# Issuing the transfers of the inverted 64-blocks from GpSimd's queue instead of SyncE's

## The chip, the core and the metric

The kernel runs on one core of a Trainium2 chip. The core has five engines with an instruction queue each: TensorE (PE; its weight loads are listed apart as PEld), ScalarE (ACT), VectorE (DVE), GpSimd (POOL) and SyncE (SP). A transfer between the chip's memory (DRAM) and the core's on-chip memory is an instruction in the queue of one engine; that engine issues it, in the order of its queue and after the waits that stand before it, and 16 DMA engines then carry it out. The metric is the device time of one execution in microseconds (us).

## What is computed

One step of a decoder of two layers, for a prompt of 512 tokens and 8 sampled tokens at once. Layer 0 mixes by a convolution and by attention; layer 1, in which the change lies, is a gated delta net with 16 query/key heads and 32 value heads. Its prompt part works on chunks of 64 tokens, 8 chunks for each value head, and for each of them it inverts a lower triangular matrix of 64 x 64:

```python
lmat = jnp.where(strict, jnp.einsum('bhnid,bhnjd->bhnij', kb, kc) * decay, 0.0)
tmat = lax.linalg.triangular_solve(lmat + eye, jnp.broadcast_to(eye, lmat.shape),
                                   left_side=True, lower=True, unit_diagonal=True)
u_val = tmat @ (vc * bc[..., None])
w_key = tmat @ (kb * jnp.exp(gc)[..., None])
# per chunk n, with state s:
v_new = u_n - w_n @ s
o_n = qd_n @ s + a_n @ v_new
s = s * gl_n[..., None, None] + jnp.swapaxes(kd_n, -1, -2) @ v_new
```

These are 32 x 8 = 256 matrices, the 64-blocks of the title. The 8 sampled tokens go through the same recurrence one step at a time, each with a state of its own (`state_delta`). All values are fp32.

## The kernel before

The weights stream from DRAM in halves of 128 x 1024 values (`wr`). ACT rounds each half to a short form `wh`, DVE takes the rest, `wl<-wr,wh`, and PE multiplies both by the activations, which are split in the same way (`uh`, `ul`), into `pg`: three products of 16 matmuls of 260 columns for a half, so that a half needs one ACT rounding and one DVE split before its last 16 matmuls.

All instructions are first recorded by a class `Sched`. Its `flush` (lines 307 to 432) then plays the recorded work through: each engine has a clock, `cost` prices an instruction, `LAT` the way from one engine to another, and whenever an engine is free it takes the ready instruction with the lowest number (an order of priority: record order plus a bias). The work is emitted in the order of the planned starts, so every engine's queue is fixed before the run. Transfers are planned on the engine "SP" (`Q` in `build`): an issue costs 340 to 1700 ns, moves on one common clock of transfers (`dma_free`), and SP is held back when that clock is over `WINDOW`, 5 us, ahead.

Layer 1 has two phases. In the first (`l1a`), `prepare(i, lk)` runs for 16 pairs of value heads, i = 0 to 15; it forms the triangular matrices `lt` of the pair and stores them, with the other matrices of the chunks, in a DRAM tile `sp` (`sv` and `spa` are views of it). Behind i = 7 the function `inverses(0, iv)` is recorded for the first eight pairs, the first half; `inverses(1, iv)`, the second half, is a generator that `background` steps forward while the next phase runs.

`inverses` works as follows. Eight loads (`m<-sp`) bring the 128 matrices of its half into a tile `m`, one matrix on each of the 128 partitions, 64 x 64 values each; a load fills 16 partitions, 256 KB, and reads rows of 64 values, so pieces of 256 bytes. DVE puts ones on the diagonals (`MEMSET m` 128x64), then inverts by steps of a multiplication into `tmp` and a sum (`TENSOR_REDUCE`), and at last clears the upper corner (`MEMSET m` 128x32x32, in the trace 128x1024). Eight stores (`sp<-m`) of 256 KB write the inverses back into the places of `lt`. There is one buffer for `m`: the second half's loads wait until the first half's stores have read it.

The second phase (`l1b`) runs for the 16 pairs: `values(i)` (a convolution, `conv_c`, with DVE's steps `cacc<-buf,conv_w_c,cacc`; GpSimd clears the first three columns of each `buf`), `z_gates(i)`, `scan(i, ...)` (it loads the inverses and the other matrices of a pair as `pk<-sp`, 448 KB, and goes through the chunks on PE: `pm`, `ct`, `at`), and `samples(i, ...)`, which loads the sampled tokens' state `S<-state_delta`, copies into one of two tiles `es` that GpSimd cleared at the phase's beginning, and multiplies `pd<-S,es`. `window` loads the small tiles `win`. The output blocks y of the pairs are stored, and towards the end they are loaded again (`m<-y_0`, `m<-y_1`, ...) into the tile `m`, which takes the place of the second half's `m` and so waits for its stores.

Lines 430 and 431 of the profile are the two lines in `flush` that emit every instruction, so its rows tell the work by tile names. The names that the text uses, apart from those above: `z<-dd` (stores of gates from a tile of the first phase; the tiles of the second phase take that room, and the clears of `es` wait for them), `zt<-z` (their loads), `oss` and `vs` (small tiles of the second phase), `kql<-` (the rest of the split of keys and queries in `prepare`), `o_ccp` and `o_ccs` (outputs: the last rows of the convolution's input).

Of the kernel before, what the change touches and what calls it, by code (L numbers as in the profile page):

```python
# [27 lines left out]
GQ = 16  # L28
# [10 lines left out]
class Sched:  # L39


    def __init__(self, tc):
        self.tc, nc = tc, tc.nc
        self.ops, self.rings, self.owner, self.hist, self.masks = [], {}, {}, {}, {}
        self.bias, self.done, self.start, self.fins, self.dma_free, self.aset = 0, 0, [], [], 0.0, 0
        self.real = {"PE": nc.tensor, "ACT": nc.scalar, "DVE": nc.vector, "POOL": nc.gpsimd, "SP": nc.sync}
        self.t = {e: 0.0 for e in self.real}
        self.cols, self.port = [0.0] * 4, {"DVE": 0.0, "POOL": 0.0}

# [192 lines left out]
    def cost(self, eng, meth, args, kw, out, ins):  # L242

        n = self.free(out)
        PSM = bass.MemoryType.PSUM
        big = [x for x in ins if not (self.free(x) == 1 and n > 1)]
        ptr = len(ins) - len(big)
        nps = sum(1 for x in ins if x.space == PSM)
        acc = kw.get("accum_out") is not None
        if eng == "PE":  # L250
            k, m = ins[0].shape[0], out.shape[0]
            rows = 32 if k <= 32 else 64 if k <= 64 else 128
            if meth == "transpose":
                return max(109 if rows == 128 else 82, 0.833 * n + 2), (rows, 128), "t"
            if ins[1].dtype == F32R:
                return (max(120, 0.417 * n + 6) if rows == 128 else 0.833 * n + 8), (rows, 128), "r"
            cols = 32 if m <= 32 else 64 if m <= 64 else 128
            if (rows, cols) == (128, 32):
                return max(100, 1.667 * n + 52), (rows, cols), "q"
            return 2 * max(109 if rows == 128 else 58, 0.833 * n + 3), (rows, cols), "f"  # L260
        if eng == "ACT":
            f = args[2] if meth == "activation" else AF.Copy
            return 0.83 * n + (58 if nps else 109) + 93 * ptr + 105 * acc, f
        if eng == "SP":
            by, run = int(4 * np.prod(out.shape)), 4096
            for x in [out] + ins:
                r = 1
                for st, c in reversed([tuple(d) for d in (x.ap if x.space == bass.MemoryType.DRAM else list(x.ap)[1:])]):
                    if st != r:
                        break  # L270
                    r *= c
                run = min(run, 4 * r)
            few = any(x.space != bass.MemoryType.DRAM and x.shape[0] <= 16 for x in [out] + ins) and by > 20000
            return (1700 if few else 340 if by / run <= 130 else 560), int(by * (1 + 77 / run if run >= 512 else 512 / max(run, 64)))
        two = sum(1 for x in big if x.space != PSM) > 1
        if eng == "DVE":
            fast = meth in ("tensor_scalar", "tensor_copy") and not nps and out.space != PSM
            if meth == "memset":
                return 0.52 * n + 60, True
            if meth == "reciprocal":  # L280
                return 6.6 * n + 70, False
            if meth == "tensor_tensor_scan":
                return 2.09 * n + 55, two
            if meth == "tensor_reduce":
                return 1.04 * self.free(ins[0]) + 65, False
            r = 0.52 if fast else 1.04
            if meth == "tensor_tensor" and n >= 100:
                inner = [[d for d in list(x.ap)[1:] if d[1] > 1] for x in big]
                if any(d and abs(d[-1][0]) > 4 for d in inner):
                    r = 1.83  # L290
            return r * n + 68 + 60 * ptr + 12 * acc, two or fast
        if meth == "tensor_tensor":
            return 1.57 * n + 430, True
        if meth == "tensor_reduce":
            return 2.1 * self.free(ins[0]) + 100, True
        if meth == "memset":
            return 0.5 * n + 130, True
        return 0.83 * n + 370 + 60 * ptr, True
# [3 lines left out]
           "ACT": {"PE": 262, "ACT": 145, "DVE": 132, "POOL": 172},  # L302
           "DVE": {"PE": 257, "ACT": 130, "DVE": 128, "POOL": 157},
           "POOL": {"PE": 205, "ACT": 77, "DVE": 70, "POOL": 90},
           "SP": {"PE": 970, "ACT": 950, "DVE": 950, "POOL": 950, "SP": 1000}}

    def flush(self):

# [8 lines left out]
        for i in range(lo, N):  # L317
            eng, deps, after = ops[i][0], ops[i][5], ops[i][8]
# [17 lines left out]
        while left:  # L336
# [10 lines left out]
            now, e = best  # L347
# [27 lines left out]
            if e == "PE":  # L375
                if c[1] != self.cfg:
                    if self.kind == "q":
                        now = max(now, max(self.cols))
                    now += self.SWITCHED if c[1] == (128, 128) else self.SWITCHES
                    self.cfg = c[1]  # L380
                elif self.kind in "tf" and c[2] == "r":
                    now = max(now - 78, ready[i])
                self.kind = c[2]
                if c[2] == "q":
                    g = self.column(ops[i])
                    start[i] = max(now, self.cols[g])
                    self.cols[g] = fin = start[i] + c[0]
                    end = start[i] + 14
                else:
                    start[i] = now  # L390
                    end = fin = now + c[0]
            elif e == "ACT":
                start[i] = now
                end = fin = now + c[0]
                s = self.SETS.get(c[1])
                if s is not None and self.aset not in s:
                    self.aset = min(s)
                    end = fin = end + 1280
            elif e == "SP":
                start[i] = now  # L400
                end = now + c[0] + 60
                self.dma_free = fin = max(self.dma_free, end + 650) + c[1] / self.RATE
            else:
                other = "POOL" if e == "DVE" else "DVE"
                if c[1]:
                    now = max(now, self.port[other])
                start[i] = now
                end = fin = now + c[0]
                if c[1]:
                    self.port[e] = end  # L410
# [12 lines left out]
        with self.tc.manual_schedule():  # L423
            for i in order:
                o = ops[i]
                s = self.SETS.get(o[6][1]) if o[0] == "ACT" else None
# [70 lines left out]
def build(tc, a, ctx):  # L497
    nc = tc.nc
    sc = Sched(tc)
    V, S, G, PE, Q = (sc.engine(e) for e in ("DVE", "ACT", "POOL", "PE", "SP"))  # L500
    PS = bass.MemoryType.PSUM
    DR = bass.MemoryType.DRAM

# [738 lines left out]
    with ExitStack() as l1:  # L1242
# [122 lines left out]
        def inverses(b8, iv):  # L1365
# [6 lines left out]
                        c0, r = 4 * (8 * b8 + i), slice(64 * blk, 64 * blk + 64)  # L1372
                        blocks.append((m[p0:p0 + 16], spa[c0:c0 + 16, r, 5 + hd, r]))
            for s, dv in blocks:
                Q.dma_start(s, dv)
            mf = m.rearrange("p j i -> p (j i)")
            V.memset(mf[:, 0::65], 1.0)
            pr = m[:, 32:64, 0:32]
# [37 lines left out]
                    yield dot(diag(0, s_, s_ + i, 1, 2 * s_, nb)[:, :, :, 0], x, prb(0, s_, 0, i + 1))  # L1416
            V.memset(pr, 0.0)
            for s, dv in blocks:
                Q.dma_start(dv, s)


        def gates(gp_):
# [518 lines left out]
```

## Time and profile before

| | us |
|---|---|
| median of three timed runs | 3222.65 |
| lowest and highest | 3216.93 and 3229.28 |
| profiled execution, its own time | 3229.8 |
| span of the trace in it | 3228.0 |
| PE busy in the span | 3072.7 (95%) |
| VectorE busy | 2346.4 (73%) |
| ScalarE busy | 1578.2 (49%) |
| GpSimd busy | 128.3 (4%) |

The profile shows one execution. Times are in us from the start of its span. A row of a timeline gives start, duration, engine (SPq is SyncE's queue of transfers), line, operation, output<-inputs and, in brackets, how long the engine was idle before it and which work ended the wait. The duration of a transfer's row on SPq is the time that its issue took; the time until its data has landed is told apart. The duration of a row of several instructions (x6) is that of all of them. PEclk is the granted clock of TensorE as a share of the full one: of the two levels of 1.2 and 2.4 GHz, 1.00 is the higher one throughout. Near 1830 us the first half's inversion ends and near 1865 us the second phase begins; near 2370 us the second half's inversion ends.

### The profile page before, as it was taken

How to read it: one execution, taken by the hardware profiler on the slowest of the kernel's cores; microseconds unless marked ns; L12 is line 12 of the kernel's file. 1: busy time of each engine (PE TensorE's matmuls, PEld its weight loads, DVE VectorE, ACT ScalarE, POOL GpSimd, SP SyncE). 2: the span in 40 equal slices, each digit the busy share in tenths (PEclk: the TensorE clock that was granted, in tenths of full speed). 3: DMA queues.
4: the chain of work that ended last, by engine and by line, in shares of the span. 5: the costliest groups of instructions: out<-in, count | busy, mean ns of one | idle time of the engine just before them, and what ended most of it. 6: DMA issues, size and time to landing. Idle time of an engine off the chain costs nothing.

```text
span 3228.0 us, 65519 instructions
## 1 busy us (share of the span) xinstructions
PE 3072.7 (95%) x24448; PEld 2800.0 (87%) x24448; DVE 2346.4 (73%) x6470; ACT 1578.2 (49%) x2942; POOL 128.3 (4%) x157
## 2 busy tenths in 40 slices
PE   8999999998979999999999979999999989999997
PEld 5798888886868886998999969999989779989997
DVE  3477988789674476676999749999956566665755
ACT  3234344433543366777773236555535555554544
POOL 0000000000001111000000000000000000001111
PEclk9999999999979999999999989999989789899998
DMA  9988898989627798687664485555364444476754
GB/s 316 296 274 292 298 313 293 327 306 316 219 89 260 287 308 276 141 168 149 151 155 135 110 153 176 154 150 168 127 180 146 137 126 154 130 247 193 227 181 137
DMA packets 361586, 667.01 MB, mean 207 GB/s; under 512 B 103698, under 2 KB 216339, under 8 KB 357171
## 3 DMA queue, kind: packets, MB, share of 16 engines
q1 hardware_dynamic: 361266, 662.82, 67.4%
q8 instruction: 192, 3.15, 0.4%
q14 instruction: 128, 1.04, 0.1%
HBM read 574.95 MB, written 87.70 MB: 205 GB/s over the span
## 4 chain that ended last, share of the span: by engine, by line
PE 84%; DVE 7%; DMA 6%; ACT 1%; SPq 1%; issue 1%; POOLq 0%; ACTq 0%; POOL 0%; DVEq 0%
PE pg L431 66%; PE pm L431 9%; PE pl L431 6%; PE pd L431 2%; SPq L431 1%; DVE wl L431 1%; DVE junk L431 1%; DMA S<-state_delta 1%; DMA page<-cache_k 1%; DMA wa<-w_ada 1%; DVE blk L431 1%; DVE acc L431 1%; DVE S L431 1%; DMA o_ds<-S 1%; DMA m<-sp 0%
## 5 line engine op out<-in xcount | busy, mean ns | idle before, releaser
L431 PE MATMUL pg<-uh,wh 128*128 128x260 f32 (+1 forms) x6112 | 1343.3, 290 | 12.5 <-ACT wh L431 6.2
L431 PE MATMUL pg<-ul,wh 128*128 128x260 f32 (+1 forms) x6112 | 1344.0, 289 | 3.0 <-DVE ul L431 2.6
L431 PEld LDWEIGHTS pg<-uh,wh 128*128 128x128 f32 (+1 forms) x6112 | 1001.0, 191 | 67.1 <-issue 46.0
L431 PEld LDWEIGHTS pg<-ul,wh 128*128 128x128 f32 (+1 forms) x6112 | 1004.0, 191 | 46.0 <-issue 33.8
L431 ACT CAST wh<-wr 128x1024 fp32r<-128x1024 f32 (+3 forms) x508 | 512.5, 1010 | 769.0 <-PE pg L431 634.2
L431 PE MATMUL pg<-uh,wl 128*128 128x260 f32 (+1 forms) x6112 | 880.6, 287 | 0.2
L431 DVE TENSOR_TENSOR wl<-wr,wh 128x1024 fp32r<-128x1024 f32 (+3 forms) x508 | 616.0, 1213 | 328.1 <-ACT wh L431 145.6
L431 PEld LDWEIGHTS pg<-uh,wl 128*128 128x128 f32 (+1 forms) x6112 | 791.6, 190 | 42.4 <-issue 37.3
L431 DVE SCALAR_TENSOR_TENSOR junk<-page,qbc 128x128 f32<-128x128 f32 x1024 | 223.2, 293 | 7.7 <-DMA page<-cache_k 4.4
L431 DVE TENSOR_TENSOR tmp<-m 128x224 f32<-128x224 f32 (+19 forms) x238 | 200.8, 844 | 4.0
L431 DVE SCALAR_TENSOR_TENSOR acc<-gp,conv_w_a,acc 128x512 f32<-128x512 f32 x240 | 181.5, 756 | 4.1 <-ACT acc L431 1.1
L431 ACT ACT_TABLE_LOAD x123 | 157.8, 1283 | 22.5 <-DVE rs L431 10.9
L431 DVE SCALAR_TENSOR_TENSOR cacc<-buf,conv_w_c,cacc 128x512 f32<-128x512 f32 x192 | 143.2, 746 | 13.8 <-ACT cacc L431 12.0
L431 DVE TENSOR_REDUCE m<-tmp 128x32 f32<-128x224 f32 (+19 forms) x238 | 131.1, 551 | 4.0
L431 DVE DVE_READ_ACCUMULATOR junk<-page,qbc 128x1 f32 x1024 | 90.2, 88 | 0.0
L431 PE MATMUL pl<-page,wst 128*32 128x512 f32 x512 | 80.2, 611 | 8.8 <-DMA page<-cache_v 8.8
L431 PE MATMUL pl<-wa,cpad 128*32 128x512 f32 x512 | 82.9, 604 | 2.7 <-DMA wa<-w_ada 2.7
L431 PE MATMUL pg<-yh,wh 128*128 128x260 f32 x320 | 79.2, 284 | 0.7 <-ACT wh L431 0.7
L431 PE MATMUL pg<-yl,wh 128*128 128x260 f32 x320 | 78.9, 283 | 0.0
L431 DVE SCALAR_TENSOR_TENSOR S<-S,egb,pl 128x128 f32<-128x128 f32 x256 | 71.9, 341 | 5.7 <-PE pl L431 5.2
L431 ACT ACTIVATE jk<-osb 128x128 f32<-128x128 f32 x128 | 39.7, 310 | 54.9 <-DVE osb L431 53.9
L430 ACT ACT_TABLE_LOAD x51 | 65.4, 1283 | 0.9
(381 smaller groups left out, 3418.8 us busy)
## 6 DMA issues: line engine op xcount, KB each, us to landing
wr<-w_in_odd SPq DMA_DIRECT2D x194, 512.0 KB, 4.6
page<-cache_k SPq DMA_DIRECT2D x128, 512.0 KB, 5.5
wa<-w_ada SPq DMA_DIRECT2D x128, 512.0 KB, 5.4
page<-cache_v SPq DMA_DIRECT2D x128, 512.0 KB, 5.7
wr<-w_out_odd SPq DMA_DIRECT2D x128, 512.0 KB, 3.7
wr<-w_in_even SPq DMA_DIRECT2D x94, 512.0 KB, 5.5
page<-w_ada SPq DMA_DIRECT2D x128, 256.0 KB, 5.0
pk<-sp SPq DMA_DIRECT2D x64, 448.0 KB, 4.0
```

Source lines behind the costliest of these rows:

```text
L430: self.tc.nc.scalar.preload_act_table_set("natural_log_exp_and_others")
L431: o[2](*o[3], **o[4])
```

## The change

The planner gets a sixth engine, "GQ", which stands for transfers issued from GpSimd's queue: a clock of its own, the price and the latencies of SP, but no holding back by `WINDOW`. In `inverses`, and only there, the eight loads and the eight stores of a half are recorded on it (`Q2`) instead of on SP (`Q`). At run time they stand in GpSimd's one queue together with its other instructions, in the planned order.

```diff
-        self.real = {"PE": nc.tensor, "ACT": nc.scalar, "DVE": nc.vector, "POOL": nc.gpsimd, "SP": nc.sync}
+        self.real = {"PE": nc.tensor, "ACT": nc.scalar, "DVE": nc.vector, "POOL": nc.gpsimd, "SP": nc.sync, "GQ": nc.gpsimd}
...
-        if eng == "SP":
+        if eng in ("SP", "GQ"):
...
-           "SP": {"PE": 970, "ACT": 950, "DVE": 950, "POOL": 950, "SP": 1000}}
+           "SP": {"PE": 970, "ACT": 950, "DVE": 950, "POOL": 950, "SP": 1000, "GQ": 1000}}
+    LAT["GQ"] = LAT["SP"]
...
-            elif e == "SP":
+            elif e in ("SP", "GQ"):
...
-    V, S, G, PE, Q = (sc.engine(e) for e in ("DVE", "ACT", "POOL", "PE", "SP"))
+    V, S, G, PE, Q, Q2 = (sc.engine(e) for e in ("DVE", "ACT", "POOL", "PE", "SP", "GQ"))
...
             for s, dv in blocks:
-                Q.dma_start(s, dv)
+                Q2.dma_start(s, dv)
             mf = m.rearrange("p j i -> p (j i)")
...
             for s, dv in blocks:
-                Q.dma_start(dv, s)
+                Q2.dma_start(dv, s)
```

With other engines and clocks the planner comes to another order at some places. On GpSimd, from the middle of the first phase on, before:

```order
L431 TENSOR_TENSOR blk<-blk,rows 128x2x260 x10
L431 MEMSET buf 128x3 x32
L431 MEMSET es_25415 128x256
L431 MEMSET es_25416 128x256
L431 MEMSET buf 128x3 x32
```

and now, up to the second half's loads:

```order
L432 MEMSET buf 128x3 x11
L432 DMA m<-sp 16x64x64 x4
L432 MEMSET buf 128x3 x8
L432 DMA m<-sp 16x64x64 x4
L432 MEMSET buf 128x3 x13
L432 DMA sp<-m 16x64x64 x8
L432 DMA m<-sp 16x64x64
L432 MEMSET es_25415 128x256
L432 MEMSET es_25416 128x256
L432 MEMSET buf 128x3 x2
L432 DMA m<-sp 16x64x64 x7
L432 MEMSET buf 128x3 x16
```

The first half's stores and one load of the second half stand ahead of the clears of `es`, and seven loads ahead of the next clear of `buf`; the second half's eight stores follow further down. The first of the second half's loads carries the wait for the stores to have landed.

On VectorE, at the beginning of the second phase, before (the copies into `es` are those of the first two pairs, `MEMSET m` is the second half's diagonal):

```order
L431 COPY es_25416<-kqd 128x8 x2
L431 TENSOR_TENSOR wl<-wr,wh 128x1024 x2
...
L431 TENSOR_TENSOR vs<-pm,snk 128x512
L431 TENSOR_TENSOR wl<-wr,wh 128x1024 x2
L431 COPY win<-pg 128x8
L431 TENSOR_TENSOR wm<-win,conv_w_c 128x64
L431 SCALAR_TENSOR_TENSOR cacc<-buf,conv_w_c,cacc 128x512
L431 TENSOR_REDUCE dv<-wm 128x16
L431 SCALAR_TENSOR_TENSOR cacc<-buf,conv_w_c,cacc 128x512 x2
L431 TENSOR_TENSOR wl<-wr,wh 128x1024
L431 TENSOR_TENSOR vs<-pm,snk 128x512
L431 MEMSET m 128x64
```

and now:

```order
L432 TENSOR_TENSOR vs<-pm,snk 128x512
L432 TENSOR_TENSOR wl<-wr,wh 128x1024
L432 MEMSET m 128x64
L432 TENSOR_TENSOR tmp<-m 128x8
...
L432 TENSOR_REDUCE m<-tmp 128x8x4
L432 COPY win<-pg 128x8
L432 TENSOR_TENSOR tmp<-m 128x200
L432 TENSOR_TENSOR wl<-wr,wh 128x1024
L432 SCALAR_TENSOR_TENSOR cacc<-buf,conv_w_c,cacc 128x512
```

The clear of `m`, which waits for all eight loads, comes behind one weight split where it came behind three, and the three `cacc` steps that were ahead of it stand behind it.

On SyncE, where the second half's stores were, before:

```order
L431 DMA wr<-w_in_odd 128x1024
L431 DMA sp<-m 16x64x64 x3
L431 DMA wr<-w_in_odd 128x1024
L431 DMA sp<-m 16x64x64 x3
L431 DMA wr<-w_in_odd 128x1024
L431 DMA sp<-m 16x64x64
L431 DMA pk<-sp 128x896 x3
```

and now:

```order
L432 DMA S<-state_delta 128x2048
L432 DMA wr<-w_in_odd 128x1024
L432 DMA pk<-sp 128x896
L432 DMA zt<-z_17859 128x520
L432 DMA m<-y_0_17875 128x260
L432 DMA m<-y_1_17876 128x260
L432 DMA wr<-w_in_odd 128x1024
L432 DMA m<-y_2_17877 128x260
```

The stores are gone from this queue; the `pk` here is that of pair 8, the first one that reads the second half's inverses (it waits for four of the stores), and the loads of y into `m` (which wait for the other four) stand close behind it, each group with a weight load after it.

## Rows read from the trace of the kernel before

**Rows 1.** The page: busy time, share of the span and instructions of each engine.

```profile
PE 3072.7 (95%) x24448; PEld 2800.0 (87%) x24448; DVE 2346.4 (73%) x6470; ACT 1578.2 (49%) x2942; POOL 128.3 (4%) x157
```

**Rows 2.** The page: the chain that ended last, share of the span by engine.

```profile
PE 84%; DVE 7%; DMA 6%; ACT 1%; SPq 1%; issue 1%; POOLq 0%; ACTq 0%; POOL 0%; DVEq 0%
```

**Rows 3.** Stretches: length; busy us (instructions) of PE, PEld, DVE, ACT, POOL; PEclk, DMA share, GB/s.

```profile
1530.00:1830.00 300.00, 298.17 (x2493) 296.45 (x2492) 294.61 (x550) 161.30 (x228) 1.11 (x11) 1.00 0.53 140
1838.00:1856.00 18.00, 18.00 (x153) 18.00 (x151) 3.67 (x3) 4.29 (x5) 0.00 (x0) 1.00 0.76 113
1875.00:1887.00 12.00, 10.35 (x86) 10.36 (x87) 5.76 (x10) 4.16 (x6) 0.00 (x0) 1.00 1.21 108
1890.00:1920.00 30.00, 15.73 (x109) 12.02 (x108) 7.46 (x19) 5.29 (x15) 0.10 (x1) 0.70 1.00 130
2400.00:2420.00 20.00, 20.00 (x101) 17.20 (x102) 1.92 (x4) 5.06 (x16) 0.20 (x2) 0.56 0.65 183
```

**Rows 4.** Timeline of SyncE's queue between the phases: start, us, operation.

```profile
1838.10 17.84 SPq L431 DMA_DIRECT2D sp<-m  x6
1856.04 5.34 SPq L431 DMA_DIRECT2D z<-dd  x2
...
1874.59 12.36 SPq L431 DMA_DIRECT2D m<-sp  x3
...
1902.92 3.05 SPq L431 DMA_DIRECT2D S<-state_delta  x1
```

**Rows 5.** Timeline of VectorE at the same place.

```profile
1832.94 0.91 DVE L431 MEMSET m<- 128x1024 f32 x1 [0.16 <-issue]
...
1851.45 1.23 DVE L431 TENSOR_TENSOR wl<-wr,wh 128x1024 fp32r<-128x1024 f32 x1 [4.55 <-PE pg L431]
...
1864.68 0.10 DVE L431 MEMSET oss<- 128x10 f32 x2 [12.01 <-DMA z<-dd]
...
1913.77 0.11 DVE L431 MEMSET m<- 128x64 f32 x1 [22.16 <-DMA m<-sp]
```

**Rows 6.** Timeline of PE at the same place.

```profile
1868.28 0.80 PE L431 MATMUL pg<-uh,wh 128*128 128x260 f32 x2 [5.37 <-ACT wh L431]
...
1887.60 2.09 PE L431 MATMUL pg<-uh,wl 128*128 128x260 f32 x16
...
1916.17 1.93 PE L431 MATMUL pd<-S,es 128*32 128x256 f32 x16 [10.33 <-DMA S<-state_delta]
```

**Rows 7.** Timeline of GpSimd: near the first loads, and between the phases.

```profile
1402.16 0.10 POOL L431 MEMSET buf<- 128x3 f32 x1 [22.19 <-DVE lt L431]
...
1864.66 0.56 POOL L431 MEMSET es<- 128x256 f32 x2 [199.57 <-DMA z<-dd]
...
1888.69 0.10 POOL L431 MEMSET buf<- 128x3 f32 x1 [23.38 <-DMA o_ccp<-buf]
```

**Rows 8.** Timelines of SyncE, VectorE and PE at the first half's last loads.

```profile
1485.83 0.33 SPq L431 DMA_DIRECT2D m<-sp  x1
...
1503.68 0.11 DVE L431 MEMSET m<- 128x64 f32 x1 [9.19 <-DMA m<-sp]
...
1507.00 0.58 PE L431 MATMUL pm<-kql,kqh 128*128 128x256 f32 x1 [7.72 <-DVE kql L431]
```

**Rows 9.** Timelines of SyncE and PE at the second half's stores.

```profile
2369.02 7.74 SPq L431 DMA_DIRECT2D sp<-m  x3
...
2390.54 3.98 SPq L431 DMA_DIRECT2D pk<-sp  x3
...
2397.10 0.42 PE L431 MATMUL pm<-ct,pk 64*64 64x64 f32 x2 [4.49 <-DMA pk<-sp]
```

**Rows 10.** Tile m: issue ns (min/median/max), starts; and KB each, us from issue to landing.

```profile
L431 SPq DMA_DIRECT2D m<-sp x16: 325/578/7287, 1383.1 to 1901.3; - x16
m<-sp SPq DMA_DIRECT2D x16, 256.0 KB, 13.9
sp<-m SPq DMA_DIRECT2D x16, 256.0 KB, 8.7
```

## The prediction

> **What bounds the kernel now.** I read the engine table first: TensorE (PE) is busy for 95% of the span [rows 1], and the chain that ended last is PE for 84% [rows 2]. A change that only moves transfers can therefore gain or lose in one way: through the stretches in which PE stands still or runs at its lower clock. The table by stretches shows which they are. From 1530 to 1830 us PE issues 2493 matmuls in 300 us, 0.12 us each, at full clock; from 1890 to 1920 it issues 109 and is busy 15.73 of 30 us at a granted clock of 0.70; from 2400 to 2420 it issues 101 where 166 would fit, at 0.56 [rows 3]. These two stretches, and a small one near 1500 us, are where the inverted blocks travel.
>
> Next the timelines of these places, engine by engine. SyncE (SP): six of the eight stores of the first half keep its queue for 17.84 us, 2.97 us each, and the last two z stores stand behind them until 1856; three loads of the second half take 12.36 us, and the load of S leaves only at 1902.92 [rows 4]. VectorE (DVE): it waits 12.01 us for the last z store, and 22.16 us, until 1913.77, for the loads of m [rows 5]. PE waits 5.37 us at 1868 for weights and 10.33 us until 1916 for S [rows 6]. GpSimd (POOL) clears es at 1864.66 and then only buf [rows 7]. The first half's loads cost DVE 9.19 and PE 7.72 us near 1500 [rows 8]; its last stores hold SP from 2369.02 to 2390.5, and PE waits 4.49 us for pk [rows 9].
>
> **The change, part by part.** 32 transfers of 256 KB leave SP: 16 loads, 16 stores, each in pieces of 256 bytes. Nothing is removed from the data path; DVE, ACT and PE do the same work. What counts are three things: the price of an issue on POOL, what now stands behind it there, and where the planner has put the dependants.
>
> *The price, g.* The trace has no transfer issued by POOL. The nearest rows are the same transfers on SP: 0.33 us at the least, 7.29 us at the most [rows 10], and 2.97 us each in the row of six [rows 4]. I take 2.97, since that is the pace at which these very pieces went through, and keep 0.33 and 7.29 as ends. A gain below 0.33 is excluded, since an issue takes some time on whatever queue. Below about 2.3 us the transfers themselves set the pace: in the stretch of stores the DMA engines were busy 0.76 of the time, so 0.76 x 2.97 = 2.26 us for a store; in the stretch of loads 108 GB/s moved, so 262 KB / 108 = 2.43 us for a load [rows 3].
>
> The Trainium skill has a price for a whole transfer on this path: "DMA: Bandwidth & Descriptors", section "Anatomy of one DMA — SWDGE (gpsimd) path", gives 2.0 us plus the bytes at 436 GB/s, which is an estimate of 2.6 us here. With it in place of 2.97 the sum below would end near 3218 us; no row of this trace shows it.
>
> *The middle, 1834 to 1920 us.* SP is rid of the stores, so the z stores and the next weights go out some 20 us earlier, and the waits of 12.01 and 5.37 us [rows 5, 6] lose their cause. But POOL now runs, in this order: eight stores, one load that waits for all eight to land, the two clears of es, two of buf, seven loads. DVE copies into es ahead of its next weight split, so PE hangs on that chain. Eight issues from 1833.85 (the end of DVE's last clear of m) end at 1833.85 + 8 x 2.97 = 1857.6; a store lands 8.7 us after issue [rows 10], so 1866.3; the first load's issue ends at 1869.3. The es clear comes about 5 us after its time of before [rows 7], while PE has some 3.9 us of matmuls that need no split weights (32 at 0.12 us). So the 5.37 us are mostly given back: POOL's in-order queue is late in SP's place.
>
> Then the second wait. Seven more issues end at 1870 + 20.8 = 1890.8, and with 8.7 us all loads have landed at M = 1899.5, some 14 us earlier than 1913.8 [rows 5]. (The loads' own median to landing is 13.9 us [rows 10], but with up to eight queued on each other; with it M is 1904.7 and 5 us more are lost.) DVE, however, meets its clear of m earlier in its own order: one weight split and three convolution steps stand behind it that stood ahead. PE then stops at the matmuls it ran at 1887.60 [rows 6]. When DVE goes on it does eleven small instructions, some 3 us (the 19 of that stretch took 7.46 us with the long ones [rows 3]), and a 1.23 us split, so PE restarts at M + 4.2. From there to where before stood at 1920 is 2.4 us up to 1890 and the 15.73 us busy after it [rows 3], 18.1 us. So 1920 of before becomes 1899.5 + 4.2 + 18.1 = 1921.8: **2 us lost**. S no longer waits behind loads; it waits behind stores of window rows that need DVE, goes out at about M + 7 and is in time for PE.
>
> *The first half, 1383 and 1486 us.* The loads wait for the lt stores as before. Four issues from 1485.83 end at 1497.7, landing by 8.7 us gives 1506.4 against 1503.68 [rows 8]; with some overlap I count **1 us lost**. At 1383 four issues take POOL until 1395, and its next clear of buf came at 1402.16 [rows 7]: hidden. At 7.29 us they would end at 1412 and the clear would be 10 us late. The clear at 1888.69 [rows 7] now stands behind seven loads until 1890.8; its readers stand behind DVE's wait anyway, so that costs nothing.
>
> *The last stores, 2369 us.* SP was held 21.5 us there. Now SP itself waits: the planner puts pk of pair 8 and the loads of y into m close behind, so SP stands until four stores land, 4 x 2.97 + 8.7 = 20.6 us, and again until all eight land, 32.5 us, with a weight load behind. PE has four weight halves in hand, 5.78 us each (a split of 1.23 us after 4.55 us of waiting for PE [rows 5]), 23 us, and I count half of the 20 us of scan matmuls after 2400 [rows 3] as work that needs no pk, 10 us. So nothing is won or lost: **0**, with a gain of 12.6 us as the other bound: the wait of 4.49 us and 20 x (1 - 101/166) = 7.8 us of low clock, rounded up.
>
> *The sum.* 2 + 1 + 0 = 3 us slower. The profiled execution took 3229.8 us, span 3228.0 and 1.8 around it; the median of the three timed runs is 3222.65, 7 us below, and differences carry over one to one. **Forecast 3222.65 + 3 = 3226 us.**
>
> **The rivals.**
>
> *POOL's issue is dear (slower).* Each half and each direction is eight issues in one in-order queue, and two blocks follow each other in the middle. At g = 5: M = 1833.85 + 40 + 8.7 + 40 + 8.7 = 1931, so 1953.6 for 1920: 34 us; the first half 4 x 5 + 8.7 = 28.7 us against 17.85, 11 us; at the end eight stores land after 48.7 us against 33 us of supply, 16 us. Together 61 us: 3284. At 7.29: M = 1968, 70 us; 20 us; 34 us; together 124: 3347. It decides from g of about 3.5, where the middle alone gives 11 us and the first half 5. For it: 1024 pieces per transfer, and that no row shows POOL's price. Against it: 2.97 us is what a queue with the same pieces needed when it was full.
>
> A rule of the Trainium skill points the same way: "SBUF — State Buffer", section "Who interferes with whom", says that VectorE and GpSimd share ports, and that a copy or tensor_scalar in a two-port mode keeps GpSimd from writing descriptors. The trace bears it out little here: DVE was busy 3.67 of 18 us in the stores' stretch and 5.76 of 12 in the loads' [rows 3], nearly all with two-operand instructions. If all of that time locked POOL out, 2.97 us would become 3.7 and 5.7, M 1927 and the time near 3255.
>
> *SP's freedom is worth all of it (faster).* If g is small and the pieces go at the transfers' own pace, M = 1833.85 + 18.1 + 8.7 + 19.4 + 5 = 1885, 1920 becomes 1907: 13 us won; with the 7.72 us of the first half and the 12.6 us of the end, 33 us: 3190 at best; 3205 if half of the last two comes. For it: SP's queue stood for 21.5 us and more at each place. Against it: each of these waits has a second one behind it, DVE's for m, which the change doesn't touch.
>
> *It doesn't do what it says* is excluded: the order of the changed program has all 32 on POOL and none on SP. That both queues feed the same transfers at the same pace is part of the forecast.
>
> **How the numbers follow.** Same within 0.5% (16 us, about what a measurement of this kernel can tell from no change): 0.47, the forecast. Dear issue: 0.36, slower. Freed queue: 0.17, faster. The range takes the fast rival nearly to its best, 3195, and the dear one to just past g = 5, 3290; beyond it is g near 7.29, which I give one in ten.
>
> **What would show it.** In the changed kernel's profile: POOL's DMA instructions and their mean time (g); the es clear near 1869; DVE's wait for m ending near 1900 with some 20 us of length; PE idle before it about as much as the 14 us of before; SP with no long issues near 1840 and 1880, but a wait for POOL's stores near the end. I am wrong if g is over 3.5 us, if the es clear is not what DVE waits for at the boundary, or if the loads land before 1890.

## The result, and the profile after

The changed kernel takes **3189.36 us** (median of four runs, 3184.64 to 3193.86), the kernel before 3221.59 beside it: a ratio of **0.9897, 95% interval 0.9873 to 0.9922**. That is 32 us faster, and outside the range of the forecast (3195 to 3290). The forecast's sign was wrong too. A traced execution can lie up to 11 us off its kernel's median (that of the kernel before, 3229.8 us, lies 7 over it), so a sum taken from one trace is no timed result.

First the page of the changed kernel: busy time by engine, the chain by engine, and two of the DMA queues (packets, MB, share of 16 engines; q1 serves SyncE, q0 GpSimd).

```profile
PE 3039.5 (95%) x24448; PEld 2777.0 (87%) x24448; DVE 2347.9 (74%) x6470; ACT 1574.6 (49%) x2942; POOL 152.8 (5%) x189
...
q1 hardware_dynamic: 327986, 654.43, 65.6%
q0 software_dynamic: 2560, 8.39, 2.6%
...
PE 83%; DVE 7%; DMA 6%; ACT 2%; issue 1%; POOL 0%; SPq 0%; POOLq 0%; ACTq 0%; DVEq 0%
```

Against [rows 1, 2] the chain is the same, but PE is busy for 33 us less with the same 24448 matmuls: they ran at a higher clock (0.976 in the mean over the span). This line is the first hint of where to look. The transfers did move: 32 of them, in 2560 packets of q0.

Next GpSimd's timeline between the phases, and the two rows of tile m that hold its issues (ns, min/median/max; first and last start).

```profile
1835.31 6.06 POOL L432 DMA_DIRECT2D sp<-m  x8 [169.04 <-DVE m L432]
1863.76 0.77 POOL L432 DMA_DIRECT2D m<-sp  x1 [22.39 <-DMA wr<-w_in_odd]
1864.73 0.56 POOL L432 MEMSET es<- 128x256 f32 x2 [0.21 <-DMA wr<-w_in_odd]
...
1865.30 5.29 POOL L432 DMA_DIRECT2D m<-sp  x7
...
L432 POOL DMA_DIRECT2D m<-sp x16: 763/764/937, 1385.3 to 1869.8; - x16
L432 POOL DMA_DIRECT2D sp<-m x16: 763/763/775, 1835.3 to 2322.2; - x16
```

An issue on GpSimd takes 0.76 us and hardly varies. The first load waits for the eight stores to land, until 1863.76 (as read from the order; its row names a weight load that landed in the same wait), and the clears of `es` stand behind it. Then VectorE and PE at the same place:

```profile
1864.76 0.10 DVE L432 MEMSET oss<- 128x10 f32 x2 [10.92 <-DMA z<-dd]
1865.08 0.49 DVE L432 COPY es<-kqd 128x8 f32<-128x8 f32 x4 [0.22 <-POOL es L432]
...
1895.78 0.11 DVE L432 MEMSET m<- 128x64 f32 x1 [18.55 <-DMA m<-sp]
```

```profile
1867.89 0.75 PE L432 MATMUL pg<-uh,wh 128*128 128x260 f32 x2 [3.83 <-ACT wh L432]
...
1894.98 0.58 PE L432 MATMUL pg<-uh,wh 128*128 128x260 f32 x1 [7.52 <-ACT wh L432]
...
1903.12 1.12 PE L432 MATMUL pm<-ct,vc 128*128 128x128 f32 x4 [7.56 <-ACT vc L432]
```

The first of PE's two stops is of another kind than was forecast: ACT had no weights to round. Its row, and the stretch of the loads (columns as in [rows 3]):

```profile
1893.88 1.04 ACT L432 CAST wh<-wr 128x1024 fp32r<-128x1024 f32 x1 [19.26 <-DMA wr<-w_in_odd]
```

```profile
1866.00:1896.00 30.00, 20.15 (x149) 19.65 (x149) 6.70 (x10) 6.73 (x10) 4.60 (x7) 0.87 1.05 113
```

The DMA engines are full (1.05) at 113 GB/s, as they were before with the loads on SyncE (1.21 at 108 [rows 3]): in both stretches the pieces of 256 bytes take them up, whichever queue issues them, and the weights wait among them (19.26 us).

The waits of [rows 5, 6] are there again, smaller or in other places: 12.01 us became 10.92, 5.37 became 3.83, 22.16 became 18.55, and PE now stops twice for 7.5 us where its longest stop was 10.33. This is near the picture that was forecast, and it holds no 32 us.

**Where the gain is.** Both kernels run the same 24448 matmuls, so the start of the n-th one in each trace can be set side by side. The time between two such starts, in us:

```
matmuls            before  after   after - before
0 to 14000         1822.3  1823.6    +1.3   layer 0, first phase
14000 to 15000      148.8   143.8    -5.0   stores and loads between the phases
15000 to 16900      231.3   238.0    +6.7   scans of pairs 1 to 5
16900 to 18900      263.2   257.2    -6.0   pairs 5 to 9, last stores
18900 to 19800      150.6   118.8   -31.8   pairs 9 to 11
19800 to 20900      131.7   131.7     0.0
20900 to 21300       57.7    51.9    -5.8   one wait for S
21300 to the end    393.8   392.8    -1.0
```

(The line before the last varies from run to run: in a second trace of the changed kernel it is 57.8. It makes 6 of the 10 us by which the two traces lie further apart, 42 us, than the medians, 32.) The pairs are numbered from 0 and told by the first matmul of their scans. Most of the gain is made at 2470 to 2625 us, some 80 us behind the last of the stores before, and some 150 us behind it now.

The n-th matmul is not the same matmul in both orders. At 14000 and at 19800 both have done the same set, at 16900 all but 4 are the same, but at 18900 the kernel before has done 56 more weight matmuls and 56 fewer of the scan and the samples. The two kinds cost PE nearly the same when nothing holds it up (0.11 to 0.12 us at the higher clock), so the row can stand; but the stretch of before holds more steps of the scan and 482 weight matmuls, that of the changed kernel 538. Between 16900 and 19800 the work is the same, but for those 4, and the gain is 37.8 us (columns as in [rows 3]; before, after):

```profile
2210.57:2624.34 413.77, 385.08 (x2903) 352.61 (x2902) 298.95 (x763) 210.51 (x553) 1.42 (x14) 0.89 0.49 146
```

```profile
2213.42:2589.35 375.93, 356.69 (x2903) 332.56 (x2902) 281.49 (x724) 210.44 (x556) 7.47 (x22) 0.96 0.56 161
```

PE stands still for 28.7 us before and 19.2 after, and is busy for 28.4 us less at a granted clock of 0.96 instead of 0.89: three quarters of the gain are the clock. The last part of it, from matmul 18900 to matmul 19800, before and after:

```profile
2473.76:2624.34 150.58, 131.87 (x903) 114.13 (x902) 93.75 (x274) 78.34 (x220) 0.51 (x5) 0.82 0.41 133
```

```profile
2470.57:2589.35 118.78, 112.30 (x903) 102.84 (x902) 79.66 (x225) 69.63 (x185) 0.51 (x5) 0.94 0.52 158
```

The same number of matmuls, of the mixture just told; PE stands still for 18.7 us before and 6.5 after, 12.2 us less, and is busy for 19.6 us less, at a granted clock of 0.94 instead of 0.82. A piece of PE's timeline of this place, in the scan of pair 11, before:

```profile
2592.38 1.23 PE L431 MATMUL pm<-r,pk 128*128 128x128 f32 x4 [0.72 <-ACT osb L431]
2594.06 0.80 PE L431 MATMUL pl<-vn,pk 128*128 128x128 f32 x2 [0.46 <-ACT vn L431]
...
2596.88 0.79 PE L431 MATMUL pm<-sth,th 128*128 128x256 f32 x2 [0.66 <-ACT sth L431]
2597.47 0.63 PE L431 MATMUL pm<-sth,tl 128*128 128x256 f32 x2
...
2599.25 1.01 PE L431 MATMUL pm<-r,pk 128*128 128x128 f32 x3 [0.72 <-ACT osb L431]
```

and, from the scan of pair 12 in the changed kernel, just behind the stretch:

```profile
2596.09 0.36 PE L432 MATMUL pm<-vdh,th 128*128 128x256 f32 x1
...
2596.75 0.40 PE L432 MATMUL pg<-uh,wh 128*128 128x260 f32 x2
2596.98 0.40 PE L432 MATMUL pg<-ul,wh 128*128 128x260 f32 x2
...
2598.07 0.40 PE L432 MATMUL pm<-sth,th 128*128 128x256 f32 x2
2598.31 0.29 PE L432 MATMUL pg<-uh,wl 128*128 128x260 f32 x1
2598.43 0.40 PE L432 MATMUL pm<-sth,tl 128*128 128x256 f32 x2
```

The scan is a chain PE, ACT, DVE, PE. Where weight matmuls (`pg`) stand between its steps, PE has work while ACT and DVE do theirs; before, here, there are none left, PE waits 0.46 to 0.72 us at each step, and the two `pm<-sth,tl` take 0.63 us, at the lower clock, instead of 0.40. How many weight matmuls stand between the first matmul of a pair's scan and the first of the next one's is a property of the planner's order:

```
from pair            7    8    9   10   11   (12 to 14: 271, 293, 344 in both)
before             572  272  203  192  101
after              337  281  287  253  191
```

Before, VectorE finishes the second half's inversion late (its last clear of `m` starts at 2368.08 us; in the changed kernel at 2315.72), pair 8 needs its result, and while PE waits for that the planner gives it 235 more weight matmuls. They are missing in the pairs behind. Told by pairs: from the first matmul of pair 7 to that of pair 8 it takes 92.9 us before and 58.0 after; pairs 8 to 11 together take 217.9 us with 768 weight matmuls before, 206.6 us with 1012 after. A pair with fewer weight matmuls is not shorter, and those that stand ahead of pair 8 cost their own time.

### The profile page after: what moved, and what is told of

The parts are those of the page before. It is cut to its first block, busy times and chain, and to the rows that moved or that the text cites. A ratio compares the mean times of both kernels' runs of the same rounds, so it can differ in the third digit from the quotient of the medians.

```text
span 3186.2 us, 65578 instructions
## 1 busy us (share of the span) xinstructions
PE 3039.5 (95%) x24448; PEld 2777.0 (87%) x24448; DVE 2347.9 (74%) x6470; ACT 1574.6 (49%) x2942; POOL 152.8 (5%) x189
## 2 busy tenths in 40 slices
DMA packets 330865, 667.01 MB, mean 209 GB/s; under 512 B 70929, under 2 KB 183570, under 8 KB 326450
## 3 DMA queue, kind: packets, MB, share of 16 engines
q1 hardware_dynamic: 327986, 654.43, 65.6%
q0 software_dynamic: 2560, 8.39, 2.6%
## 4 chain that ended last, share of the span: by engine, by line
PE 83%; DVE 7%; DMA 6%; ACT 2%; issue 1%; POOL 0%; SPq 0%; POOLq 0%; ACTq 0%; DVEq 0%
PE pg L432 66%; PE pm L432 9%; PE pl L432 6%; PE pd L432 2%; DMA m<-sp 1%; DVE junk L432 1%; DMA wa<-w_ada 1%; DVE wl L432 1%; DVE acc L432 1%; DMA page<-cache_v 1%; DMA S<-state_delta 1%; DMA page<-cache_k 1%; DVE S L432 1%; DVE blk L432 1%; DMA o_ds<-S 0%
## 5 line engine op out<-in xcount | busy, mean ns | idle before, releaser
L432 PE MATMUL pg<-uh,wh 128*128 128x260 f32 (+1 forms) x6112 | 1339.2, 289 | 17.8 <-ACT wh L432 12.2
L432 DVE DVE_READ_ACCUMULATOR junk<-page,qbc 128x1 f32 x1024 | 81.2, 79 | 0.0
```

The costliest lines, as they stand in the source:

```text
L432: o[2](*o[3], **o[4])
```

## The experiments

The theory, **F**: the order is what counts, and of it this shortage of weight matmuls. Its rivals: **Q**, SyncE's freed queue is the cause; **E**, the earlier place of the second half's loads, in the pairs up to 7.

**1. Order and queue apart.** Three kernels and the changed one again, on one chip. In the first, the planner makes the changed order but the transfers are emitted on SyncE:

```diff
-        ... "SP": nc.sync, "GQ": nc.gpsimd}
+        ... "SP": nc.sync, "GQ": nc.sync}
```

In the second, the planner of before makes its own order, and only the emitted instruction is GpSimd's (loads and stores both go through this):

```diff
+        Q2 = lambda o, x: sc.record("SP", "dma_start", nc.gpsimd.dma_start, (o, x), {})
```

PE's and VectorE's instructions stand in exactly the order of the changed kernel in the one, of the kernel before in the other. The third plans and issues only the second half's stores on GpSimd:

```diff
-                Q2.dma_start(s, dv)
+                Q.dma_start(s, dv)
...
-                Q2.dma_start(dv, s)
+                (Q2 if b8 else Q).dma_start(dv, s)
```

> The changed kernel once more, for the comparison on one chip with the three others. Both theories: 3189 us, 0.990 of the kernel before. A place for the gain is expected as in the first trace of it: PE's matmuls 18900 to 19800 (pairs 10 and 11 of the second phase) some 30 us shorter than before.

> The order of the changed kernel, word for word on PE and VectorE, but its 32 transfers stand in SyncE's queue at their planned places. Theory P (the planner's new order of the second phase makes the gain, whatever queue issues the transfers): 0.990, about 3190 us, with matmuls 18900 to 19800 as short as in the changed kernel. Theory Q (SyncE's freed queue makes the gain): 1.000, about 3222 us. Between: the queue's part is what is missing to 0.990.

> The order of the kernel before, word for word on PE, VectorE and ScalarE, with the 32 transfers taken out of SyncE's queue and put at their places into GpSimd's. Theory P: 1.000, about 3222 us, within 0.3% (10 us), with the two stretches of the blocks (1834 to 1920 and 2369 to 2420 us) up to some 10 us shorter. Theory Q: 0.990, about 3190 us.

> Only the second half's eight stores are planned and issued on GpSimd; the 24 others are on SyncE. The order on PE is that of the kernel before up to matmul 17000 and another behind it. Theory Q: the gain of freeing SyncE at the last stores alone, at most 12.6 us by the forecast's bound, 0.996 to 1.000. Theory P: whatever the other order behind 17000 does to PE's idle time in pairs 10 to 12 decides: 0.990 if it fills that time, 1.000 if not; the stretch up to matmul 16900 is equal to before within 2 us.

Measured: the changed kernel again 0.9907 (0.9888 to 0.9926), its order on SyncE **0.9914** (0.9896 to 0.9932), the old order on GpSimd **0.9996** (0.9982 to 1.0010), the last stores alone 0.9964 (0.9946 to 0.9981). The stretch of matmuls 18900 to 19800 in the kernel with the changed order on SyncE, and in the one with the old order on GpSimd:

```profile
2475.06:2593.08 118.02, 111.54 (x902) 102.17 (x901) 79.65 (x225) 69.62 (x185) 0.50 (x5) 0.96 0.53 159
```

```profile
2478.38:2628.94 150.56, 131.82 (x903) 114.07 (x901) 93.77 (x274) 78.12 (x220) 0.50 (x5) 0.82 0.42 133
```

The stretch follows the order to a microsecond and does not care for the queue. Q has fallen: what made the kernel faster is that a planner that counts the transfers on a clock of their own comes to another order of the whole second phase; moving them to another queue is worth -1.3 us, between -6 and +3. The last stores alone shift the counts a little (585, 270, 192, 192, 101 from pair 7 on) and win some 11 us; in the trace this stretch is 10 us shorter (140.5). The counts do not explain that part: they are nearly those of before. PE's order does differ from before at 796 places, all between matmuls 18374 and 19645, and PE stands still for 14.9 us of the stretch instead of 18.7, at a clock of 0.85: where the weight matmuls stand within a pair counts too. One expectation failed: up to matmul 16900, where the order is that of before, matmuls 14000 to 16900 took 375.7 us against 380.1, not within 2 us. So a stretch of one trace is good to some 4 us.

**2. The same counts without the change, and the counts spoilt within it.** The pace of the second half's inversion is a number in the code of before:

```diff
-                background(6000)
+                background(5000)
```

With 5000, and with 3000, the order has the changed kernel's counts from pair 8 on (with 3000, 270 instead of 281 at pair 8), with all transfers on SyncE and the loads of the second half where they were. In the third kernel the first half goes back to SyncE (`(Q2 if b8 else Q)` for loads and stores). The fourth is the changed kernel, with the second half's stores made dear in the planner alone:

```diff
+                if b8:
+                    sc.record("GQ", "dma_start", nc.gpsimd.dma_start, (dv, s), {}, cost=(8000, 262144))
+                else:
+                    Q2.dma_start(dv, s)
```

> The kernel before with one number changed: the second half's inversion is recorded at a pace of 5000 instead of 6000 for each pair; all 32 transfers stay on SyncE and the planner has no sixth engine. Of this order the weight matmuls between the first matmuls of neighbouring pairs are, from pair 7 on, 328, 281, 287, 253, 191, as in the changed kernel from pair 8 on (337, 281, 287, 253, 191) and unlike the kernel before (572, 272, 203, 192, 101). Theory F (pairs 9 to 12 run their scans with too few weight matmuls beside them when pair 8 starts late; that is the whole gain): 0.990, 3190 us, with matmuls 18900 to 19800 in 118 us as in the changed kernel instead of 150.6. Theory E (the earlier loads of the second half, that is pairs 0 to 7, make the gain): 1.000, since the loads stand where they stood.

> The same with a pace of 3000: 339, 270, 287, 253, 191 from pair 7 on. Theory F: 0.990 or somewhat better, 3180 to 3190 us, since the pairs before 8 have more matmuls beside them than in the changed kernel. Theory E: 1.000.

> The changed kernel with the first half's 16 transfers back on SyncE; the second half's 16 on GpSimd, in a plan of its own (328, 281, 287, 253, 191 from pair 7 on). Theory F: 0.990 to 0.993 (pairs 1 and 2 stall a little more than in the changed kernel). If the first half's transfers made part of the gain: 0.993 to 0.997.

> The changed kernel, its 32 transfers on GpSimd; in the planner alone the second half's eight stores cost 8 us of its clock each, so it has the pairs behind 8 start later and use up more weight matmuls first: 337, 357, 272, 270, 113 from pair 7 on instead of 337, 281, 287, 253, 191. Until matmul 18000 the order is nearly that of the changed kernel. Theory F: part of the gain is lost, by the 78 weight matmuls that pair 11 lacks: 78 x 0.12 = 9 us and as much again by the lower clock, so 9 to 18 us over the changed kernel, 0.993 to 0.996. Theory E: as the changed kernel, 0.990.

Measured: pace 5000 **0.9936** (0.9915 to 0.9958), pace 3000 0.9938 (0.9915 to 0.9960), the second half alone **1.0008** (0.9993 to 1.0023), pair 8 late 0.9925 (0.9900 to 0.9950). By stretches, with the changed kernel's second trace beside them (us):

```
matmuls            before  after2  pace5000  pace3000  2nd half  late
14000 to 15000      148.8   144.1     146.0     148.1     151.2  141.7
15000 to 16900      231.3   238.7     241.2     236.1     240.3  238.7
16900 to 18900      263.2   255.3     259.5     267.8     276.5  256.9
18900 to 19800      150.6   117.7     118.5     117.1     118.1  127.3
sum                 793.8   755.8     765.3     769.1     786.0  764.6
```

The stretch of 18900 to 19800 is settled as far as the order goes: 117 to 119 us in each kernel with 281 (or 270), 287, 253, 191, whether its transfers are on SyncE, on GpSimd or on both, against 150.6. In all of these PE's order from matmul 18539 on is the same, matmul for matmul, so they show what this order does and not what the counts alone do. With 113 instead of 191 at pair 11 it is 127.3, 9.6 us more (9 were expected from the 78 matmuls, up to 18 with the clock); the timed ratio of that kernel, 0.9925, is just under the 0.993 to 0.996 that were expected and not clear of the changed kernel's. E has fallen with the two paces: the loads stood where they were and 20 us came nonetheless.

But F as stated, that this is the whole gain, has fallen too. The second half alone has the good stretch and gives most of it back elsewhere: against before it loses 13.3 us in 16900 to 18900 and 11.4 in 14000 to 16900 (391.5 against 380.1), which leaves 7.8 of the 32.5 us in this trace and nothing in the timed ratio. The paces pay back 4 to 9 us in the same way. The changed kernel gains because its order is good in pairs 9 to 11 and pays little ahead of them (7 us in matmuls 15000 to 16900, which it has back in the stretches beside).

**3. What was lost at the last stores.** Two further pairs of one order on two queues, and one more plan:

```diff
-                background(6000)
+                background(3000)
...
-                Q.dma_start(s, dv)        (and the stores)
+                Q2(s, dv)                 (record("SP", ...) with nc.gpsimd.dma_start, as above)
```

the second half's kernel with `"GQ": nc.sync`, and the changed kernel with `WINDOW = 3000.0`.

> The order of the pace of 3000, word for word on PE and VectorE, with the 32 transfers put from SyncE's queue into GpSimd's at their places. In its run on SyncE the last stores held that queue and PE waited 9.44 us at 2372 for work behind them, and then ran at the lower clock. If a freed SyncE is worth something where the order has a scan right behind the stores: 10 us off the last stretch (matmuls 16900 to 18500 in 209 us instead of 218.8), 0.990 to 0.991. If the transfers delay the others in the same way from either queue: 0.994 as on SyncE.

> The order of the kernel with the second half on GpSimd, which measured 1.001, word for word on PE and VectorE, with all 32 transfers on SyncE. If that kernel lost at the last stores because GpSimd's transfers slowed SyncE's issues (8.06, 6.27 and 5.86 us for two each at 2306 to 2332, where they took 0.4 us elsewhere): 0.996 to 0.998, matmuls 17500 to 17700 in 40 to 45 us instead of 53.9. If its order is what loses: 1.000, with 54 us there; with the stores in front of pk in SyncE's queue also longer.

> The changed kernel with the planner's limit on transfers ahead at 3 us instead of 5, an order of its own in the whole kernel; 328, 281, 287, 253, 191 weight matmuls between the pairs from pair 7 on. Theory F gives the stretch of matmuls 18900 to 19800 in 118 us; the rest of an order is not foreseen by it, so the time lies between 0.985 and 1.000, and below 0.990 it beats the changed kernel.

Measured: pace 3000 on GpSimd 0.9923 (0.9895 to 0.9951), the second half's order on SyncE 0.9997 (0.9981 to 1.0014), the limit of 3 us 0.9937 (0.9916 to 0.9958). None beats the changed kernel. The limit of 3 us has the good stretch as F foretold (116.8 us, with 118 expected) and loses in 16900 to 18900 (271.6). With pace 3000, PE's longest wait behind the stores, on SyncE and on GpSimd:

```profile
2371.97 0.69 PE L431 MATMUL pd<-ct,qs 128*128 128x128 f32 x2 [9.44 <-DVE qs L431]
```

```profile
2365.91 0.69 PE L431 MATMUL pd<-ct,qs 128*128 128x128 f32 x2 [6.37 <-DVE qs L431]
```

The wait fell by 3 us. Of the ten microseconds that were hoped for in matmuls 16900 to 18500, 4.6 came (218.8 to 214.2), hardly more than the 4 us to which such a stretch is good; the timed ratios are not apart. The order of the second half's kernel shows the other side. Its stores on GpSimd, with SyncE, VectorE and PE beside them:

```profile
2309.92 6.09 POOL L432 DMA_DIRECT2D sp<-m  x8 [25.86 <-DVE r L432]
```

```profile
2314.63 6.27 SPq L432 DMA_DIRECT2D o_dp<-st  x2
2321.00 2.55 SPq L432 DMA_DIRECT2D kw<-krd  x1
2323.64 2.45 SPq L432 DMA_DIRECT2D o_ds<-S  x1
2326.18 5.86 SPq L432 DMA_DIRECT2D y<-y  x2
```

```profile
2338.39 0.68 DVE L432 TENSOR_TENSOR kx<-kw,ct 32x512 fp32r<-32x512 f32 x1 [12.40 <-DMA kw<-krd]
```

```profile
2339.82 0.66 PE L432 MATMUL pm<-pk,ba 64*64 64x64 f32 x4 [8.97 <-DVE vs L432]
```

After eight issues of 0.76 us GpSimd is done, but SyncE's own issues take 2.5 to 3.1 us each while the stores are carried out, and the small load `kw`, issued behind them, keeps VectorE for 12.40 us and PE for 8.97 (PE's row names `vs`, which stands right behind it on VectorE). (The 8.06 us that the expectation counts with them are two issues of 0.33 us, at 2306.53 and 2314.26, with a wait between.) With the same order on SyncE the stores stand between these transfers in one queue; the issue of `kw` takes 3.09 us there too, but it costs VectorE only 3.28 us, and PE waits 6.56 us for S instead:

```profile
2321.28 0.68 DVE L432 TENSOR_TENSOR kx<-kw,ct 32x512 fp32r<-32x512 f32 x1 [3.28 <-DMA kw<-krd]
...
2341.40 1.93 PE L432 MATMUL pd<-S,es 128*32 128x256 f32 x16 [6.56 <-DMA S<-state_delta]
```

Matmuls 17500 to 17700 took 43.7 us there instead of 53.9, within the 40 to 45 that were expected, and yet the whole kernel measured 0.9997, not 0.996 to 0.998: the place was right, but the queue is not what this order loses. Over matmuls 14000 to 19800, four orders on SyncE and on GpSimd:

```
order                SyncE   GpSimd         timed ratio: SyncE   GpSimd
before               793.8    793.8                     (1)      0.9996
changed              758.4    755.8, 757.7              0.9914   0.9907, 0.9897
pace 3000            769.1    761.3                     0.9938   0.9923
second half alone    782.1    786.0                     0.9997   1.0008
```

The queue is worth -8 to +4 us in these sums and nothing that the timed ratios can tell, the order 35 (a sum is that of one trace). The Trainium skill has this as a rule, in "DMA: Bandwidth & Descriptors", section "Issuing engines are not separate DMA queues": transfers of all issuing engines interleave on the same 16 DMA engines, and issuing from several saves only the sequencer's time of the issue. The four pairs agree with it, and the rows of `kw` show what it means for a small transfer behind large ones.

## Why the prediction was wrong

- **What bounds the kernel** was read rightly as PE's idle and slow stretches, but only three were looked at, those where the moved transfers are [rows 3 to 9]. The stretch that decided most, at 2474 to 2624 us, has the same signs in the trace of before (18.7 us idle, clock 0.82) and was not in the argument.
- **The step that failed** is "DVE, ACT and PE do the same work. What counts are three things", whose third, "where the planner has put the dependants", was followed only at those places. PE's order in the changed kernel differs at some 4500 of its 24448 places, all from the beginning of the second phase on; the counts of weight matmuls between the pairs could have been read from it without a time. What the runs showed in its place: the new order alone, with every transfer on SyncE, takes 0.9914 of the time, 28 us less, and from matmul 16900 to 19800, where the sum has no term but the 0 of the last stores, it takes 37.8 us less.
- **The price g** was 0.76 us, not 2.97; the low end of 0.33 was nearer. It mattered little, because the transfers set the pace, as the text held possible: the first load, which waits for all eight stores, went out 28.4 us after 1835.31, 3.55 us for each, where 8 x 2.97 + 8.7 = 32.5 was forecast; the 2.26 each that had been worked out as the transfers' own pace was too low. The rival of a dear issue fell by it.
- **The middle** came near in time and in part for other reasons. The clears of `es` came at 1864.73 (forecast near 1869), and PE's wait went from 5.37 to 3.83 us, so it was "mostly given back". But VectorE waited 10.92 us for the z store and 0.22 us for `es`: the z store had left SyncE at 1853.19, some 5 us earlier than before and not 20, and its landing ended VectorE's wait at 1864.76, as before at 1864.68. That `es` is not what VectorE waits for is one of the text's own signs of being wrong. The loads landed at M = 1895.78 (forecast 1899.5), and DVE waited 18.55 us for them (some 20). But PE stopped at 1887.5 already, 8 us before that wait's end, for weights that had not landed among the loads; this collision was not in the text, which had the weights some 20 us early. Over matmuls 14000 to 15000 the changed kernel gains 5.0 us where 2 were to be lost; with its order on SyncE it gains 3.8, with the old order on GpSimd 1.5.
- **The first half**: forecast 1 us lost. VectorE's and PE's waits of 9.19 and 7.72 us [rows 8] became 9.52 and 8.05 in the changed kernel, 10.32 and 8.86 with the old order on GpSimd. Right.
- **The last stores**: forecast 0. With the old order on GpSimd matmuls 16900 to 18900 took 265.3 us against 263.2, which is 0 within the noise. In the changed kernel they took 257.2: PE's wait of 4.49 us for `pk` and the low clock behind it [rows 9, 3] are all but gone there, so 6 us of the gain that the text gave as the other bound came. That bound, 4.49 + 7.8, is 12.3 us, not 12.6.
- **The sum** of +3 us is thus what moving the transfers alone was to cost; measured with the old order it is -1.3 us (-6 to +3). As a forecast of the changed kernel it left out the term of the order, 32 us in the stretch of pairs 9 to 11.
- **The rival "SP's freedom is worth all of it"** named 3190, almost the measured time, by a mechanism that the runs refute: the first kernel of experiment 1 has no freed queue and is as fast. A fitting number did not make it right.

The rule on VectorE's and GpSimd's shared ports ("SBUF — State Buffer", section "Who interferes with whom", of the Trainium skill), which was weighed as a danger, left no mark here: 32 issues took 763 ns in the median and 937 at most. (No run here shows an instruction of that kind beside an issue by itself.) What stays open: what the number of weight matmuls does apart from their places within a pair (the last stores alone won 10 us in the late stretch with nearly the counts of before), and which of the planner's single choices makes an order lose in matmuls 16900 to 18900.

## What to carry to other kernels

Where a planner or a list scheduler sets the order, a change to one resource in its model can change the order everywhere behind, and that can outweigh the change itself, here 28 us to some 1: build the kernel with the order changed and the hardware not, and the reverse, before a gain is put down to the hardware. Before a forecast, compare the whole order on the engine that bounds the kernel, not only at the place of the edit, and ask where its filler work, which hides a serial chain, runs out. A kernel whose order has one such bad stretch can be helped by changes of the plan that have nothing to do with each other, and the next plan may lose the gain again at another place: of six other plans here five measured 0.9925 to 0.9964 and one 1.0008. And before the n-th instruction of two orders is compared, make sure that the same work lies behind it.

## What the runs showed of the hardware

- The issue of a transfer of 256 KB in pieces of 256 bytes took 0.33 to 7.29 us on SyncE [rows 10] and 0.76 to 0.94 us on GpSimd. GpSimd's went as 2560 packets, 80 for each transfer, while the packets under 512 bytes fell from 103698 to 70929, by 1024 for each.
- The DMA engines' time for them did not fall with the packets: 2.6% of 16 engines over 3186 us, that is 41 us for each transfer, or 2.6 us on all 16; on SyncE's queue 85.6 us of span-time went (67.4% of 3228.0 less 65.6% of 3186.2), 43 us for each.
- With the second half alone on GpSimd, SyncE's issues took 2.5 to 3.1 us each while the eight stores were carried out; the issue of `kw` took 0.33 us in the median elsewhere. With the same order on SyncE it took 3.09 us at this place too, and in the changed kernel no issue of SyncE took over 2.33 us while the last eight stores were carried out: it is no property of the queue alone.
- Short waits are dear through the clock: between matmuls 16900 and 19800, the same work but for 4 matmuls, 9.5 us less of standing still went with 28.4 us less of busy time, at a granted clock of 0.96 instead of 0.89 (a mean of the two levels). In the stretch of pairs 9 to 11 before, at 0.82, PE's longest wait was 2.7 us and most were under 1.
